# Reciprocal root mean squares by a full-precision matmul, a square root and a Newton step on every row

## Chip, cores and metric

The kernel runs on one core of a Trainium2 chip. The metric is the device time of one execution in microseconds. The time before is the median of three runs; one further execution was profiled, and all rows below come from it.

## What is computed

The reference is one inference step of a two-layer hybrid encoder for 1024 prompt tokens and 8 x 16 sample tokens, 1152 rows of width 1024. Layer 0 is attention, layer 1 a gated convolution; each is followed by a SwiGLU feed-forward block, and there is a final norm. The five norms are all of this form:

```
def rms_norm(x, g):
    xf = x.astype(jnp.float32)
    y = xf * lax.rsqrt(jnp.mean(xf * xf, axis=-1, keepdims=True) + EPS)
    return (y * g.astype(jnp.float32)).astype(x.dtype)
...
for i in range(DEPTH):
    hp = rms_norm(xp, norm_mix[i])
    ...  # attention (i = 0) or gated convolution (i = 1)
    xp = xp + mp
    xp = xp + swiglu(rms_norm(xp, norm_ffn[i]), w_ffn_gate[i], w_ffn_up[i], w_ffn_down[i])
y_prompt = rms_norm(xp, norm_final)
```

What matters here is the factor 1/sqrt(mean + EPS), one number per token. The kernel keeps activations transposed: features on the 128 partitions (eight tiles for 1024 features), tokens along the free dimension. So the mean of squares is a sum across partitions, and its root is needed on all 128 partitions, as a row of token factors that is the same on each.

## The kernel before, in words

All large products are done in three passes of a split format: `hi` and `lo` parts in fp32r, `hi*hi + hi*lo + lo*hi`. ScalarE makes `hi` (lines 187, 856), VectorE makes `lo` (lines 188, 857). A matmul group writes one PSUM bank; tags of banks are `g` (6) and `n` (2) after the attention, and `g` 2, `s` 3, `t` 2, `v` 1 in it (lines 714 and 1275).

**First norm** (lines 723 to 736): three blocks of 384 tokens. For each, eight tiles are loaded, split (`norm_tile`) and squared and added (`norm_sum`), and then `norm_end` makes the row of roots `rb`. The roots are applied after the projection (lines 328, 329, 348, 353), so products begin before the roots are there. The rotary tables are multiplied by them.

**Boundaries.** Between the attention output and the gates of layer 0, between the down projection and the convolution, and between the convolution's output and the gates of layer 1, `pairs` (line 1154) finishes x, makes the operands of the next products and squares x (`square`, line 929). Then `roots` (line 939) puts work into `self.late`, a list with a countdown in ticks; `tick` (line 163) is called once after each group of products. Sums come at tick 6, the spreading at tick 15.

The next products are in `unit` (line 995): two weight matrices at once by a seven-product scheme, for two halves s of the tokens, so 14 ticks per unit. The products are named by their right operand: `t2`, `b11`, `t1`, `b21`, `t3`, `b22`, `t4` (`ORDER`, line 969). In the first unit of a stage the root is not there yet, so the order is slightly different and the multiplication with the root (`rest`, line 1065) is put off until `spread` calls it, one tick into the second unit. Two wide tiles per half (`zg`, `zu`) hold a unit's result, with three buffers each. The copy of line 1037 writes into such a tile; the product `b21` writes to the same bank after that copy has read it.

**Last norm** (`down_last`, line 1224): blocks of 512, 384 and 256 tokens. After a block's eighth tile its root is made, with countdowns of 2 and 3 ticks for the first two blocks and at once for the last; `final` (line 1244) scales the eight tiles of the block and stores them.

How a root is made before: a matmul with a column of ones puts the sums with tokens on partitions (`sums`, line 233; one fp32 matmul per 128 tokens), VectorE makes the reciprocal root on a few columns by an integer guess and three Newton steps (`rstd`, line 240), the result is split and multiplied into identity matrices on ScalarE and GpSimd (`diagonals`, line 252; in `roots` lines 954 and 955), and two fp32r matmuls with ones spread the diagonals over all partitions (`spread`, line 271), from where ScalarE copies them (lines 227, 962). The per-head norm of the differential attention (`subln`, line 683) uses the same functions.

The order on each engine is not simply that of the source. The toolchain lays the instructions out ahead, by what it expects to be ready, and works in the order of the source where several are; on the chip each engine then keeps its order.

Of the kernel before, what the change touches and what calls it, by code (L numbers as in the profile page):

```python
# [11 lines left out]
F32 = mybir.dt.float32  # L12
F32R = mybir.dt.float32r
I32 = mybir.dt.int32
AF = mybir.ActivationFunctionType
ALU = mybir.AluOpType
# [3 lines left out]
P = 128  # L20
D = 1024
# [12 lines left out]
EPS = 1e-6  # L34
# [9 lines left out]
XW = SEQ + 2 + DB * (DS + 2)  # L44
PACE = 4.25
LAG = 8
SUMS = 6
SPREAD = 15
DLAG = 16
SLAG = 10  # L50
NLAG = 15
ETAG = {"sq": "ot", "ssq": "se", "diag": "pT", "rb": "rb"}
TURN = 6
RBUFS = {"st": 6, "k": 2, "q": 2, "v": 4, "pT": 2, "ot": 2, "kc": 1, "vc": 1, "se": 3, "os": 2, "ks": 1, "qbd": 2, "vn": 1,
         "smask": 1, "bmask": 1, "rb": 3}
# [44 lines left out]
class K:  # L100
# [24 lines left out]
    def early(self, name, dt=F32):  # L125

        return self.get(ETAG[name], name, (P, BLK), dt)

# [4 lines left out]
    def consts(self):  # L133
        nc, i, cp = self.nc, self.i, self.cp
        self.ident = cp.tile([P, P], F32, name="ident")
        make_identity(nc, self.ident)
        self.ones = cp.tile([P, 1], F32, name="ones")
        nc.vector.memset(self.ones, 1.0)
        self.onesr = cp.tile([P, P], F32R, name="onesr")
        nc.vector.tensor_scalar(self.onesr, self.ident, 0.0, 1.0, ALU.mult, ALU.add)  # L140
        self.g = cp.tile([P, 5, KT], F32, name="gains")
        nc.sync.dma_start(self.g, i["gains"])
        self.gn = cp.tile([P, 5, KT], F32, name="gainsn")
        nc.vector.tensor_scalar(self.gn, self.g, -1.0, None, ALU.mult)
# [47 lines left out]
    def norm_sum(self, st, m, b, xb):  # L192
        nc = self.nc
        tp = st["tmp"][b]
        sq = tp("sq")
        nc.scalar.activation(sq, xb, AF.Square)
        if st["new"] is None:
            nc.scalar.activation(xb, xb, AF.Copy, scale=self.g[:, st["gi"], m:m + 1])
        if st["acc"][b] is None:
            st["acc"][b] = sq  # L200
        else:
            acc = tp("ssq")
            nc.vector.tensor_tensor(acc, st["acc"][b], sq, ALU.add)
            st["acc"][b] = acc
        if m == KT - 1:
            if st["early"]:
                self.norm_end(st, b)()
            elif b < NB - 1:
                self.late.append([2, lambda: self.late.append([3, self.norm_end(st, b)])])
            else:  # L210
                rest = self.norm_end(st, b)
                while self.late:
                    self.late.pop(0)[1]()
                rest()

    def norm_end(self, st, b):

        tp = st["tmp"][b]
        n = st["acc"][b].shape[-1] // P
        ps = self.sums(st["pp"], st["tag"], st["acc"][b])  # L220
        r = self.rstd(ps[:, :n], D, *[self.tmp(t, (P, 4))[:, :n] for t in "vty"])
        dg = self.diagonals(r, tp)

        def rest():
            q = self.spread(st["pp"], st["tag"], dg)
            rb = st["rb"][b] = tp("rb")
            self.nc.scalar.copy(rb, q)
            if "then" in st:
                st["then"](b, q, rb)

        return rest

    def sums(self, pp, tag, sq):

# [595 lines left out]

    def small(self, name, n, dt=F32):

        bufs = {"sq": 4, "ssq": 4, "rb": 3, "diag": 2}[name]
        at = {"sq": 0, "ssq": 4, "rb": 8, "diag": 12}[name] + self.turn.get(name, 0) % bufs
        self.turn[name] = self.turn.get(name, 0) + 1
        t = self.bits[at // 2][:, at % 2 * HALF:at % 2 * HALF + n]
        return t if dt == F32R else t.bitcast(F32)
# [23 lines left out]

    def begin_sides(self, gi, pp, first, spill=False):

        return {"gi": gi, "pp": pp, "t": {}, "ssq": None, "first": first, "spill": spill, "split": None, "rest": None}

    def side(self, st, p, z, need=False):

# [70 lines left out]

    def roots(self, st):

        nc = self.nc

        def sums():
            ps = self.psum(st["pp"], "n")
            for j in range(9):
                nc.tensor.matmul(ps[:, j:j + 1], st["ssq"][:, j * P:(j + 1) * P], self.ones[:, 0:1], start=True, stop=True)
            r = self.rstd(ps[:, :9], D, *[self.tmp(t + "9", (P, 9)) for t in "vty"])
            parts = self.tmp("rp9", (P, 2, 9), F32R)
            nc.vector.tensor_copy(parts[:, 0], r)
            nc.vector.tensor_tensor(parts[:, 1], r, parts[:, 0].bitcast(F32), ALU.subtract)  # L950
            dg = [self.row("diag", F32R) for _ in range(2)]
            for j in range(9):
                c = slice(j * P, (j + 1) * P)
                nc.scalar.activation(dg[0][:, c], self.ident, AF.Copy, scale=parts[:, 0, j:j + 1].bitcast(F32))
                nc.gpsimd.tensor_scalar(dg[1][:, c], self.ident, parts[:, 1, j:j + 1].bitcast(F32), 1.0, ALU.mult, ALU.mult)
            self.late.append([SPREAD - SUMS, lambda: spread(dg)])

        def spread(dg):
            rb = st["rb"] = self.row("rb")
            for b in range(NB):  # L960
                c = slice(b * BLK, (b + 1) * BLK)
                nc.scalar.copy(rb[:, c], self.spread(st["pp"], "n", [t[:, c] for t in dg]))
            for do in st["rest"]:
                do(rb)

        self.late.append([SUMS, sums])


    ORDER = (("s2", "t2", "b"), ("a11", "b11", "a"), ("s1", "t1", "c"), ("a12", "b21", "a"), ("s3", "t3", "b"), ("s4", "b22", "c"), ("a22", "t4", "b"))
# [25 lines left out]
    def unit(self, pp, st, weights, by, end, last=False):  # L995

        nc = self.nc
        first = "rb" not in st
        if st["split"] is not None:
            split, raws = st["split"]  # L1000
            st["split"] = None
        else:
            split, raws = self.left_sides(*weights)
        order = self.ORDER
        zone, zg, zu = {}, [None, None], [None, None]
        tail = lambda s: slice(HALF + s * SUB, HALF + (s + 1) * SUB)
        vt = nc.vector
# [21 lines left out]
        for n in seq:  # L1029
            wn, p, zn = order[n]  # L1030
            for s in range(2):
                products(n, s, range(4) if not first or n > 2 else range(2 if n == 1 else 3, 4))
                ps = zone[zn, s]
# [30 lines left out]
        if first:  # L1064
            def rest(s, rb):
                nc.vector.tensor_tensor(zg[s], zg[s], self.cols(rb, s), ALU.mult)
                nc.gpsimd.tensor_tensor(zu[s], zu[s], self.cols(rb, s), ALU.mult)
                end(s, zg[s], zu[s])

            st["rest"] = [lambda rb, s=s: rest(s, rb) for s in range(2)]  # L1070
            st["rb"] = None

    def cols(self, t, s):

# [149 lines left out]
    def down_last(self, pp, x, wsrc, chunks):  # L1224

        nc, o = self.nc, self.o
# [7 lines left out]
        for j in range(KT // 2):  # L1234
            hi, lo = (self.take(n)[0][:, :2 * nk * P].rearrange("p (k c) -> p k c", c=P) for n in ("wh", "wl"))
            for z in range(2):
                w[j + 4 * z] = part = hi[:, z * nk:(z + 1) * nk, :], lo[:, z * nk:(z + 1) * nk, :]
                self.halve(*part, self.raw(wsrc[-1][j, z]))
        self.bits = [self.take("bits")[0] for _ in range(7)]
        cut = (0, 512, 896, T)  # L1240
        self.turn = {}
        st = self.begin_norm(4, None, pp, "n", {})
# [11 lines left out]
        for b in range(NB):  # L1254
            c = slice(cut[b], cut[b + 1])
            st["tmp"][b] = lambda name, dt=F32, n=cut[b + 1] - cut[b]: self.small(name, n, dt)
            for m in range(KT):
                ps = self.psum(pp, "g", (P, 512))[:, :cut[b + 1] - cut[b]]
# [147 lines left out]
```

## Time and profile before

| | us |
|---|---|
| median of 3 runs | 2657.38 |
| lowest, highest | 2656.47, 2662.86 |
| the profiled execution | 2656.52 |
| its span in the trace | 2654.7 |
| TensorE (PE) busy | 2590.6 |
| VectorE (DVE) busy | 1687.6 |
| ScalarE (ACT) busy | 944.9 |
| GpSimd (POOL) busy | 519.9 |
| mean granted TensorE clock | 0.992 of full speed |

Around the span lie 1.8 us. Busy times are of engines that run side by side; PE's matmuls overlap, so that the distance between the starts of two tells what one costs, and its duration tells less. The mean granted clock is an average over the span; a stretch at the lower level is seen only in a table by windows. In the order of time, the first norm lies in the first 56 us, the boundaries at about 713, 1488 and 1871 us, the last norm from 2610 us to the end.

### The profile page before, as it was taken

The page shows a single profiled execution, that of the slowest core. Times are in us where ns is not written, and L with a number is a line of the kernel's source. Part 1 is how long each engine was busy: PE and PEld are TensorE (multiplying, and loading weights), DVE is VectorE, ACT ScalarE, POOL GpSimd, SP SyncE. Part 2 cuts the span into 40 slices and gives each one's busy share as a digit, 9 for nine tenths or more (in the row PEclk, how much of TensorE's full clock was granted, in tenths as well). Part 3 has the DMA queues.
Part 4 walks back from the last instruction along what each step waited for, and adds up shares of the span by engine and source line. Part 5 has one row for each costly group of instructions (what it writes and reads, how often), then busy time and mean ns, then how long its engine had stood idle before and what let it go on. Part 6 is the DMA issues. An engine that isn't in the chain of part 4 may idle for free. (4 is left out here: it accounts for less than half of the span.)

```text
span 2654.7 us, 45342 instructions
## 1 busy us (share of the span) xinstructions
PE 2590.6 (98%) x17440; PEld 2548.5 (96%) x17440; DVE 1687.6 (64%) x3564; ACT 944.9 (36%) x1801; POOL 519.9 (20%) x621
## 2 busy tenths in 40 slices
PE   7999999999999999999999999999999999999997
PEld 6999999999899999999999999999999999999996
DVE  7667766677966666666326877777766666663325
ACT  6555445454532222233213422224422222222214
POOL 3434233321022222220000122210222222210002
PEclk9999999999999999999999999999999999999999
DMA  6655555662032222226212222262322222253211
GB/s 207 185 168 157 172 182 163 178 216 81 21 97 75 75 74 73 74 88 204 67 46 75 63 81 67 67 203 91 121 75 75 75 75 75 75 177 128 71 37 72
DMA packets 183577, 285.73 MB, mean 108 GB/s; under 512 B 38977, under 2 KB 107457, under 8 KB 183361
## 3 DMA queue, kind: packets, MB, share of 16 engines
q1 hardware_dynamic: 183360, 282.84, 33.6%
q8 instruction: 137, 2.24, 0.4%
q14 instruction: 80, 0.65, 0.1%
HBM read 206.67 MB, written 76.10 MB: 107 GB/s over the span
## 5 line engine op out<-in xcount | busy, mean ns | idle before, releaser
L856 ACT CAST h<-r 128x512 fp32r<-128x512 f32 x552 | 337.8, 618 | 1021.6 <-PE ps_g L1020 425.2
L857 DVE TENSOR_TENSOR l<-r,h 128x512 fp32r<-128x512 f32 x552 | 398.5, 725 | 137.2 <-ACT h L856 127.4
L1168 PE MATMUL ps_g<-yl,h 128*128 128x384 f32 x1152 | 387.7, 337 | 5.0 <-DVE yl L857 4.2
L1167 PE MATMUL ps_g<-yh,h 128*128 128x384 f32 x1152 | 387.2, 337 | 1.6 <-ACT yh L856 1.1
L1169 PE MATMUL ps_g<-yh,l 128*128 128x384 f32 x1152 | 386.9, 336 | 0.0
L1180 DVE TENSOR_TENSOR x<-ps_g,x 128x384 f32<-128x384 f32 x240 | 129.5, 553 | 211.5 <-PE ps_g L1169 211.1
L1052 POOL TENSOR_TENSOR g<-g,rb 128x288 f32<-128x288 f32 x98 | 82.1, 842 | 735.2 <-DVE g L1050 714.7
L1168 PEld LDWEIGHTS ps_g<-yl,h 128*128 128x128 f32 x1152 | 216.5, 188 | 6.9 <-DVE yl L857 6.8
L1167 PEld LDWEIGHTS ps_g<-yh,h 128*128 128x128 f32 x1152 | 216.6, 188 | 2.7 <-ACT yh L856 1.7
L1169 PEld LDWEIGHTS ps_g<-yh,l 128*128 128x128 f32 x1152 | 216.8, 188 | 0.0
L156 PE MATMUL ps_g<-hh,h 128*128 128x384 f32 x544 | 195.2, 359 | 12.7 <-ACT hh L187 6.9
L157 PE MATMUL ps_g<-hl,h 128*128 128x384 f32 x544 | 186.8, 343 | 0.6 <-DVE hl L188 0.6
L978 DVE TENSOR_TENSOR r<-r,r 128x512 f32<-128x512 f32 x224 | 153.3, 687 | 51.4 <-DMA r<-in_w_cin 22.5
L158 PE MATMUL ps_g<-hh,l 128*128 128x384 f32 x544 | 185.7, 341 | 0.0
L1056 POOL TENSOR_TENSOR u<-u,rb 128x576 f32<-128x576 f32 x98 | 156.0, 1592 | 111.5 <-DVE u L1008 107.4
L1086 DVE TENSOR_TENSOR g<-g,u 128x576 f32<-128x576 f32 x88 | 66.5, 758 | 120.1 <-POOL u L1056 120.1
L1008 DVE SCALAR_TENSOR_TENSOR u<-ps_g,u 128x288 f32<-128x288 f32 x224 | 100.2, 452 | 64.2 <-PE ps_g L1021 64.1
L1019 PE MATMUL ps_g<-tb21h,h 128*128 128x288 f32 x448 | 132.5, 296 | 5.4 <-ACT u L1037 5.4
L1019 PE MATMUL ps_g<-tt4h,h 128*128 128x288 f32 x448 | 132.2, 295 | 3.2 <-DVE u L1008 3.2
L1020 PE MATMUL ps_g<-tb11l,h 128*128 128x288 f32 x448 | 132.2, 295 | 1.6 <-DVE tb11l L886 1.6
L1019 PE MATMUL ps_g<-tt3h,h 128*128 128x288 f32 x448 | 133.6, 298 | 0.0
L1021 PE MATMUL ps_g<-tt3h,l 128*128 128x288 f32 x448 | 133.3, 298 | 0.0
(270 smaller groups left out, 7313.0 us busy)
## 6 DMA issues: line engine op xcount, KB each, us to landing
r<-in_w_gu SPq DMA_DIRECT2D x176, 256.0 KB, 2.7
y<-yd SPq DMA_DIRECT2D x52, 576.0 KB, 4.8
yd<-g SPq DMA_DIRECT2D x96, 288.0 KB, 2.6
r<-in_w_down SPq DMA_DIRECT2D x88, 256.0 KB, 2.6
r<-in_w_in SPq DMA_DIRECT2D x48, 256.0 KB, 3.4
r<-in_w_cin SPq DMA_DIRECT2D x48, 256.0 KB, 2.7
xd<-x SPq DMA_DIRECT2D x16, 576.0 KB, 3.0
x<-xd SPq DMA_DIRECT2D x16, 576.0 KB, 6.0
```

The costliest lines, as they stand in the source:

```text
L156: nc.tensor.matmul(ps, wh, xh, start=(j == 0), stop=False)
L157: nc.tensor.matmul(ps, wh, xl, start=False, stop=False)
L158: nc.tensor.matmul(ps, wl, xh, start=False, stop=(j == n - 1))
L856: self.nc.scalar.copy(hi, raw)
L857: self.nc.vector.tensor_tensor(lo, raw, hi.bitcast(F32), ALU.subtract)
L978: nc.vector.tensor_tensor(t, x_, y, ALU.add)
L1019: nc.tensor.matmul(ps, w[0][:, k, :], hi, start=(new and k == 0), stop=False, skip_group_check=True)
L1021: nc.tensor.matmul(ps, w[1][:, k, :], hi, start=False, stop=(k == 3), skip_group_check=True)
L1056: nc.gpsimd.tensor_tensor(zu[s], zu[s], self.cols(by()[1], s), ALU.mult)
L1167: nc.tensor.matmul(ps, w[q][0][:, e, :], ys[k][0][0][:, c], start=(k == 0), stop=False, skip_group_check=True)
L1168: nc.tensor.matmul(ps, w[q][0][:, e, :], ys[k][1][0][:, c], start=False, stop=False, skip_group_check=True)
L1169: nc.tensor.matmul(ps, w[q][1][:, e, :], ys[k][0][0][:, c], start=False, stop=(k == nk - 1), skip_group_check=True)
```

## The change

The sum of squares is multiplied by a 128x128 matrix of 1/1024 in a full-precision (fp32) matmul, which gives the mean on all partitions at once. ScalarE takes the square root of mean + EPS, VectorE its reciprocal r, and one Newton step follows: r * (1.5 - 0.5 * (mean + EPS) * r * r). All of it is done on whole rows of the block, 128 partitions by up to 512 tokens. `subln` keeps the old way. At a boundary the three blocks are done at tick 10, and `rest` is called at the end of the first unit. In the last norm, `final` is called by `norm_end` itself, the countdown of 3 is gone, and the last Newton operation of a block may write to PSUM, from where ScalarE copies it for GpSimd.

```
-SUMS = 6
-SPREAD = 15
+ROOTS = 10
...
+        self.over = cp.tile([P, P], F32, name="over")
+        nc.vector.memset(self.over, 1.0 / D)
+        self.eps = cp.tile([P, 1], F32, name="eps")
+        nc.vector.memset(self.eps, EPS)
...
             if st["early"]:
-                self.norm_end(st, b)()
+                self.norm_end(st, b)
             elif b < NB - 1:
-                self.late.append([2, lambda: self.late.append([3, self.norm_end(st, b)])])
+                self.late.append([2, lambda: self.norm_end(st, b)])
...
     def norm_end(self, st, b):
+        rb = st["rb"][b] = st["tmp"][b]("rb")
+        if "then" in st:
+            st["then"](b, self.root(st["pp"], st["tag"], st["acc"][b], rb, True), rb)
+        else:
+            self.root(st["pp"], st["tag"], st["acc"][b], rb)
+
+    def root(self, pp, tag, sq, r, spare=False):
+        nc = self.nc
+        ps, t = (self.psum(pp, tag, (P, 512))[:, :sq.shape[-1]] for _ in range(2))
+        nc.tensor.matmul(ps, self.over, sq, start=True, stop=True)
+        nc.scalar.activation(r, ps, AF.Sqrt, bias=self.eps[:, 0:1], scale=1.0)
+        nc.vector.reciprocal(r, r)
+        nc.vector.scalar_tensor_tensor(t, ps, EPS, r, ALU.add, ALU.mult)
+        nc.vector.scalar_tensor_tensor(t, t, -0.5, r, ALU.mult, ALU.mult)
+        q = ps if spare else r
+        nc.vector.scalar_tensor_tensor(q, t, 1.5, r, ALU.add, ALU.mult)
+        if spare:
+            nc.scalar.copy(r, q)
+        return q
...
     def roots(self, st):
         def sums():
-            ps = self.psum(st["pp"], "n")
-            for j in range(9):
-                nc.tensor.matmul(ps[:, j:j + 1], st["ssq"][:, j * P:(j + 1) * P], self.ones[:, 0:1], start=True, stop=True)
-            r = self.rstd(ps[:, :9], D, *[self.tmp(t + "9", (P, 9)) for t in "vty"])
...
             rb = st["rb"] = self.row("rb")
             for b in range(NB):
                 c = slice(b * BLK, (b + 1) * BLK)
-                nc.scalar.copy(rb[:, c], self.spread(st["pp"], "n", [t[:, c] for t in dg]))
-            for do in st["rest"]:
-                do(rb)
-        self.late.append([SUMS, sums])
+                self.root(st["pp"], "n", st["ssq"][:, c], rb[:, c])
+        self.late.append([ROOTS, sums])
...
-            st["rest"] = [lambda rb, s=s: rest(s, rb) for s in range(2)]
-            st["rb"] = None
+            for s in range(2):
+                rest(s, st["rb"])
```

## Rows read from the trace of the kernel before

**Rows 1.** The page's first part: busy time, share of the span, instructions.

```profile
PE 2590.6 (98%) x17440; PEld 2548.5 (96%) x17440; DVE 1687.6 (64%) x3564; ACT 944.9 (36%) x1801; POOL 519.9 (20%) x621
```

**Rows 2.** Waits of PE, 0 to 70 us: sum, times, longest.

```profile
PE ps_t L275 <- POOL diag L267: 3.4, 2, 2.2
PE ps_t L275 <- ACT diag L265: 2.1, 2, 1.6
```

**Rows 3.** Timeline of PE at B1: start, us, instruction, idle before and its releaser.

```profile
710.08 0.40 PE L1019 MATMUL ps_g<-tb21h,h 128*128 128x288 f32 x1 [2.34 <-ACT u L1037]
...
713.08 3.97 PE L946 MATMUL ps_n<-ones,ssq 128*128 128x1 f32 x18 [0.76 <-DVE ssq L937]
```

**Rows 4.** Table by windows at B1: busy time by engine, then the granted clock.

```profile
705.00:710.00 5.00, 2.45 (x17) 1.99 (x15) 5.00 (x7) 3.57 (x8) 0.00 (x0) 1.00 0.00 0
...
715.00:720.00 5.00, 5.00 (x23) 5.00 (x24) 1.72 (x7) 0.00 (x0) 0.00 (x0) 0.50 0.00 0
```

**Rows 5.** Timelines of PE and DVE in the tail, in order of time.

```profile
2634.16 0.89 PE L275 MATMUL ps_n<-bits,onesr 128*128 128x384 f32 x2 [1.35 <-ACT bits L265]
2635.60 3.80 DVE L1250 TENSOR_TENSOR x<-x,ps_n 128x384 f32<-128x384 f32 x8 [0.33 <-ACT bits L227]
2642.28 0.58 PE L237 MATMUL ps_n<-ones,bits 128*128 128x1 f32 x4 [3.58 <-DVE bits L203]
2647.66 1.74 DVE L1250 TENSOR_TENSOR x<-x,ps_n 128x256 f32<-128x256 f32 x5 [1.97 <-ACT bits L227]
```

**Rows 6.** Timeline of PE at B2.

```profile
1487.79 2.06 PE L946 MATMUL ps_n<-ones,ssq 128*128 128x1 f32 x18
1489.71 0.38 PE L1019 MATMUL ps_g<-tb21h,h 128*128 128x288 f32 x1
...
1496.17 0.29 PE L1019 MATMUL ps_g<-tb22h,h 128*128 128x288 f32 x1
...
1504.12 0.86 PE L275 MATMUL ps_n<-diag,onesr 128*128 128x384 f32 x4
...
1505.20 0.61 PE L275 MATMUL ps_n<-diag,onesr 128*128 128x384 f32 x2
1505.65 0.30 PE L1021 MATMUL ps_g<-tt2h,l 128*128 128x288 f32 x1
...
1514.96 0.29 PE L1019 MATMUL ps_g<-tb21h,h 128*128 128x288 f32 x1
```

**Rows 7.** Groups of instructions by line and shape: busy us, mean ns | idle before.

```profile
L638 PE MATMUL ps_s<-kc,qbd 128*32 128x256 f32 x128 | 10.8, 391 | 0.8 <-DMA kc<-in_ck 0.8
L156 PE MATMUL ps_g<-yh,wh 128*128 128x256 f32 x32 | 9.1, 283 | 0.0
L248 DVE TENSOR_TENSOR t<-t,v 128x9 f32<-128x9 f32 x9 | 1.4, 161 | 0.0
L353 DVE TENSOR_TENSOR z<-ps_g,rb 128x384 f32<-128x384 f32 x24 | 13.3, 553 | 3.2 <-PE ps_g L158 2.7
L1085 ACT ACT_TABLE_LOAD x1 | 1.3, 1283 | 0.0
```

**Rows 8.** Instructions of tile rc: duration ns min/median/max, first and last start.

```profile
L483 DVE RECIPROCAL rc<-sm x128: 144/162/167, 80.7 to 623.1; 128x1 f32<-128x1 f32 x128
...
L522 DVE TENSOR_TENSOR rc<-rc,lam x32: 140/159/915, 84.5 to 341.5; 128x1 f32<-128x1 f32 x32
```

**Rows 9.** B2: timelines of ACT and DVE, then busy time in one window.

```profile
1505.85 0.48 ACT L962 COPY rb<-ps_n 128x384 f32<-128x384 f32 x1 [0.32 <-PE ps_n L275]
1506.36 2.67 DVE L1066 TENSOR_TENSOR g<-g,rb 128x576 f32<-128x576 f32 x2 [2.36 <-ACT rb L962]
1511.11 0.40 ACT L1037 COPY u<-ps_g 128x288 f32<-128x288 f32 x1 [0.21 <-DVE xi L1112]
...
1494.25:1506.33 12.08, 12.08 (x90) 11.89 (x89) 7.70 (x22) 6.98 (x17) 4.02 (x9) 1.00 0.26 87
```

More of the change, by code (lines that the diff above doesn't have):

```diff
@@ L51 @@
 NLAG = 15
-ETAG = {"sq": "ot", "ssq": "se", "diag": "pT", "rb": "rb"}
+ETAG = {"sq": "ot", "ssq": "se", "rb": "rb"}
 TURN = 6
@@ L206, in norm_sum @@
             if st["early"]:
-                self.norm_end(st, b)()
+                self.norm_end(st, b)
             elif b < NB - 1:
-                self.late.append([2, lambda: self.late.append([3, self.norm_end(st, b)])])
+                self.late.append([2, lambda: self.norm_end(st, b)])
             else:
-                rest = self.norm_end(st, b)
                 while self.late:
                     self.late.pop(0)[1]()
-                rest()
+                self.norm_end(st, b)
     def norm_end(self, st, b):
[L218 to L231, printed above, removed]
+        rb = st["rb"][b] = st["tmp"][b]("rb")
[16 more added lines that the diff above has]
+        return q
     def sums(self, pp, tag, sq):
@@ L831, in small @@
     def small(self, name, n, dt=F32):
-        bufs = {"sq": 4, "ssq": 4, "rb": 3, "diag": 2}[name]
-        at = {"sq": 0, "ssq": 4, "rb": 8, "diag": 12}[name] + self.turn.get(name, 0) % bufs
+        bufs = {"sq": 4, "ssq": 4, "rb": 3}[name]
+        at = {"sq": 0, "ssq": 4, "rb": 8}[name] + self.turn.get(name, 0) % bufs
         self.turn[name] = self.turn.get(name, 0) + 1
@@ L862, in begin_sides @@
     def begin_sides(self, gi, pp, first, spill=False):
-        return {"gi": gi, "pp": pp, "t": {}, "ssq": None, "first": first, "spill": spill, "split": None, "rest": None}
+        return {"gi": gi, "pp": pp, "t": {}, "ssq": None, "first": first, "spill": spill, "split": None}
     def side(self, st, p, z, need=False):
@@ L939, in roots @@
     def roots(self, st):
-        nc = self.nc
         def sums():
-            ps = self.psum(st["pp"], "n")
-            for j in range(9):
-                nc.tensor.matmul(ps[:, j:j + 1], st["ssq"][:, j * P:(j + 1) * P], self.ones[:, 0:1], start=True, stop=True)
-            r = self.rstd(ps[:, :9], D, *[self.tmp(t + "9", (P, 9)) for t in "vty"])
[L948 to L958, printed above, removed]
             rb = st["rb"] = self.row("rb")
@@ L1004, in unit @@
         order = self.ORDER
+        if first:
+            st["rb"] = None
         zone, zg, zu = {}, [None, None], [None, None]
@@ L1238, in down_last @@
                 self.halve(*part, self.raw(wsrc[-1][j, z]))
-        self.bits = [self.take("bits")[0] for _ in range(7)]
+        self.bits = [self.take("bits")[0] for _ in range(6)]
         cut = (0, 512, 896, T)
```

## The prediction

> **What bounds the kernel now.** I read the page first: TensorE (PE) is busy 98% of the span, VectorE (DVE) 64% [rows 1]. So an engine matters only where it makes PE wait, or at the two ends, where PE has nothing to do. Four kinds of place are touched: the first norm, the three boundaries, the last norm, and the clock.
>
> The waits of PE in the first 70 us are the second view: the matmuls that spread the roots wait 3.4 us for GpSimd's half of the diagonals and 2.1 us for ScalarE's, 5.5 us in all [rows 2].
>
> Third, the boundaries. There are three: attention to gates (about 713 us, B1), down to conv (1488 us, B2), conv to gates (1871 us, B3). At B1 PE is already starved before the sums: 2.34 us of waiting in one place [rows 3], and 2.45 us of work in the five from 705 to 710 us, after which the granted clock is 0.50, the lower of the two levels, 1.2 instead of 2.4 GHz [rows 4]. At B2 and B3 PE has work throughout (a row for B2 comes below).
>
> Last, the tail: from the last sums (2642.28 us) to the last scaling (2647.66 us) runs a pure chain through DVE, ScalarE, GpSimd and PE [rows 5].
>
> **PE work at a boundary.** Removed at B2: the sums hold PE from 1487.79 us to the next product at 1489.71, 1.9 us; between 1504.12 and 1505.65 us the six spreading matmuls take 1.26 us beside two ordinary products [rows 6]. Together 3.1 us. Added: three fp32 matmuls of 384 columns. The trace has fp32 of 256 columns: two records each, 391 ns against 283 ns for an fp32r record of the same width [rows 7]. Two records at 0.117 + 0.108 us are 0.45 us, 0.67 us at 384 columns, so 2.0 us in all. Net -1.1 us at B2 and at B3. At B1 the sums took 3.97 us at the low clock, after a wait of 0.76 us [rows 3]. If other products now run at the low clock in their place, I gain 1.1 us; if not, 4.0 us. I take 2.0, nearer the first, since what starved PE before 711 us is untouched. Sum of this part: **-4.2 us**.
>
> **The path of the roots at a boundary.** Removed from DVE: 14 operations of 9 columns (0.16 us each [rows 7]), and nine diagonals each on ScalarE and GpSimd. Added to DVE, per block of 384: one reciprocal and three scalar-tensor-tensor operations. The latter are priced by the 128x384 operation from PSUM, 0.55 us each [rows 7]. The trace has reciprocals of one column only: median 162 ns, 159 ns for a product of one column, and minima of 144 and 140 ns [rows 8]. From below, a reciprocal is an ordinary operation, R = 0.55 us for 384 columns. From above: the slowest (167 ns) stands 8 ns over the median product, and were that all paid per column, 384 x 8 ns + 0.55 = 3.6 us. I take the 4 ns of the minima: R = 384 x 4 ns + 0.55 = **2.1 us**, for 256 columns about 1.45.
>
> When are the roots needed? Before the change, at B2, they are complete at 1505.85 + 0.48 = 1506.33 us; DVE waits 2.36 us for them. The rest of the first unit follows, frees its wide tiles, and the copy of the next unit's product ends at 1511.51 us; PE reads behind that copy at 1514.96 us, 3.45 us later [rows 6, 9]. With the change the tenth tick comes 1.9 us sooner than the trace has it (1496.17 us), at 1494.25, as the sums are gone, and PE is 1.1 us ahead. So the roots may come 12.1 + 3.45 - 1.1 = 14.4 us after the tick without PE waiting.
>
> How long will they take? First matmul, square root (priced as the 480 ns copy of the same shape [rows 9]) and handing over: 1.4 us. The tag has two banks, so a block's matmul must wait until the block before has read its sum: a period of R + 0.55 + 0.67 + 0.5 + 0.3 = R + 2.0 us, twice. Last block: R + 1.65 us. DVE's other work gets in between: it was busy 7.70 of the 12.08 us up to the roots, through which PE was busy without a gap [rows 9], about 6 us of it not the removed operations, and I charge half, 3.0 us. Sum: 3R + 10.0 = 16.4 us, 2.0 us too late. I use the same for B1 and B3: **+6.0 us** of PE waiting.
>
> The first unit's rest moves from the fifteenth tick to the end of that unit. It issues what it issued before: one DVE and one GpSimd product per half, Silu or the conv's products, and two stores on SP. In the program these now stand ahead of the second unit's weight loads, the place that every other unit's stores have, so I price it at nothing; the cover is the five raw buffers, and a late load would cost PE what the DMA takes.
>
> ScalarE gets a table load wherever Sqrt follows another table's function: about four in the first 80 us, one each at B1, B3 (for Silu) and the tail. The trace has two, 1.283 us each [rows 7]. ScalarE waits just ahead of most of these, so I count none. The Trainium skill ("ScalarE: Activation LUTs", What ACT_TABLE_LOAD costs) has 2.66 us with a drain, and advises batching by set; our row shows 1.283 and no drain. By the page one unhidden load per boundary would add 2.7 us each, by the row 1.3.
>
> **First norm.** The 5.5 us of waits end, and 1.0 us of spreading matmuls (six at 0.17 us start to start). What is late next: the last block's inputs and DVE, busy there and burdened by three times R + 1.65 us. I take **-4.0 us**, between 0 and -6.5.
>
> **Last norm.** PE's wait of 1.35 us for block 1's diagonals ends. Block 1's eight scalings on DVE (3.80 us, from 2635.60 us), which hold up the last additions, can start about two us sooner: matmul at 2627.3, +0.67 +0.5 +2.1, three operations with others between to 2633.3. The final chain was 5.4 us (2642.28 to 2647.66) [rows 5]; now fp32 matmul at the low clock 0.9, square root 0.5, R 1.45, three operations 1.4, the copy 0.4: 4.7 us. Block 0's longer DVE work and GpSimd's overlap may take some back: **-2.5 us**, between 0 and -4.
>
> **Sum.** -4.0 - 4.2 + 6.0 - 2.5 = -4.7 us on the profiled execution's 2656.5 us, so 2651.8. The median shown is 0.9 us higher, so I say **2652.5 us**. A measurement of this kernel can tell about 0.3%, 8 us, from no change; this is within it.
>
> **Rivals.**
>
> *Cheap reciprocals.* R = 0.55 us: the roots take 11.7 us, inside the 14.4, no waiting at the boundaries. Start -4.5, PE -4.2, tail -3.5: -12.2 us, **2645 us**. For it: the medians differ by 3 ns only. Against it: both minima and medians differ in the same direction.
>
> *Dear reciprocals, the slower end.* R = 3.6 us: the roots take 20.8 us after the tick, and PE waits 6.4 us at each boundary for the second unit's zones. It decides from R = 1.5 us, where 3R + 10.0 passes 14.4. Start -2.5, PE -4.2, waits +19.3, tail -1.5: +11.1 us, **2668 us**; a fall of the clock as at B1 would come on top. The Trainium skill ("VectorE: DVE Perf Modes", the walkthrough's section on the fixed hardware budget) says that Reciprocal runs an iterative divide with a repeat count of 8; no run here shows a wide one, and at eight cycles a column that is an estimate of 3.2 us, near this rival.
>
> *The banks stop PE.* PE works in order. If the second and third fp32 matmul stand right behind the first, each holds all products behind it until DVE has read the bank: 3.5 us and R + 2.0 - 0.67 = 3.4 us, 6.9 us per boundary in place of 2.0. Total about +10 us, **2668 us**, and up to 5 us more per boundary if the clock falls (ten us at half rate, as at B1). Against it: the third spreading pair at B2 was put behind two products [rows 6], so the order is laid out with the bank's release in view.
>
> **How the numbers follow.** Forecast 0.42, cheap 0.23, dear 0.20, banks 0.15. Faster than 2649.4 us: 0.30 of the forecast, 0.8 of cheap: 0.31. Slower than 2665.4 us: 0.07 of the forecast, 0.6 of dear, 0.65 of banks: 0.25. Same: the remaining 0.44. The range is 2641 to 2674 us: it leaves out the best of cheap reciprocals with a full gain at the start, and the falls of the clock at all boundaries.
>
> **What would show it.** A 128x384 reciprocal of 2.1 us and one of 1.45 us at 256; rb complete about 16 us after tt3's last product at B2 and B3; PE waiting some 2 us for the copy at the second unit's tb21 or for a bank; no wait at the matmuls of the first norm; last scaling some 2.5 us sooner, against the end of the products. I am wrong if the reciprocal is beyond 3 us, if PE stops at the fp32 matmuls themselves, or if a low clock follows a boundary other than B1.

## The result, and the profile after

The changed kernel takes **2686.91 us** (median of 6 runs, 2685.06 to 2691.07) where the kernel before, on the same chip, takes 2656.93 us (2651.16 to 2662.86): a ratio of 1.0119, 95% interval 1.0106 to 1.0131, or 30 us more. The prediction was 2652.5 us, within 2641 to 2674. The profiled execution took 2685.66 us (span 2683.9 us) against 2656.52 us (span 2654.7 us) before.

The page's first part says almost nothing of it. To be read against [rows 1]:

```profile
PE 2591.2 (97%) x17350; PEld 2539.8 (95%) x17350; DVE 1727.5 (64%) x3500; ACT 943.0 (35%) x1767; POOL 497.0 (19%) x576
```

TensorE's work is the same within 0.6 us; DVE has 40 us more and still reads 64%. The new operation itself, by its line (columns: count, duration in ns as minimum, median and maximum, first and last start, shapes):

```profile
L233 DVE RECIPROCAL rb<-rb x12: 2537/2552/2555, 17.8 to 1905.1; 128x384 f32<-128x384 f32 x12
L233 DVE RECIPROCAL bits<-bits x3: 1754/2540/3343, 2642.8 to 2673.2; 128x512 f32<-128x512 f32 x1, 128x384 f32<-128x384 f32 x1, 128x256 f32<-128x256 f32 x1
```

A 128x384 reciprocal takes 2.55 us, where I had taken 2.1. Now who waits. TensorE's waits over the whole span (sum, times, longest):

```profile
PE ps_g L1012 <- ACT h L865: 17.3, 5, 6.2
...
PE ps_g L1014 <- DVE l L866: 7.2, 3, 2.6
...
PE ps_n L231 <- DVE bits L206: 6.4, 2, 5.3
```

The first two are new, one long and one shorter wait at each boundary: 24 us. L865 and L866 are the two halves of a split weight, `h` and `l`. So TensorE doesn't wait for roots, or for anything that a root holds up. It waits for *weights*. The timeline of PE at B2 says which (start, us, instruction, and the idle time before it with its releaser):

```profile
1497.54 0.81 PE L231 MATMUL ps_n<-ssq,over 128*128 128x384 f32 x2
...
1505.67 0.81 PE L231 MATMUL ps_n<-ssq,over 128*128 128x384 f32 x2
...
1511.23 0.81 PE L231 MATMUL ps_n<-ssq,over 128*128 128x384 f32 x2
...
1518.38 0.61 PE L1012 MATMUL ps_g<-tt2h,h 128*128 128x288 f32 x1 [4.88 <-ACT h L865]
...
1524.25 0.61 PE L1014 MATMUL ps_g<-tt2h,l 128*128 128x288 f32 x1 [2.62 <-DVE l L866]
```

TensorE goes through the three fp32 matmuls without a wait. It stops at the products with `tt2`: the first of the second unit, whose weight `s2` is a sum of three blocks that DVE must add (L969) before ScalarE can cast it (L865) and DVE can split off the rest (L866). DVE's timeline in the same stretch shows what these adds stand behind:

```profile
1501.79 2.54 DVE L233 RECIPROCAL rb<-rb 128x384 f32<-128x384 f32 x1
...
1505.11 0.68 DVE L969 TENSOR_TENSOR r<-r,r 128x512 f32<-128x512 f32 x1
...
1507.13 2.55 DVE L233 RECIPROCAL rb<-rb 128x384 f32<-128x384 f32 x1
...
1512.69 2.55 DVE L233 RECIPROCAL rb<-rb 128x384 f32<-128x384 f32 x1 [0.47 <-ACT rb L232]
...
1515.93 0.68 DVE L969 TENSOR_TENSOR r<-r,r 128x512 f32<-128x512 f32 x1
...
1517.00 0.68 DVE L969 TENSOR_TENSOR r<-r,r 128x512 f32<-128x512 f32 x1
...
1518.18 2.65 DVE L1059 TENSOR_TENSOR g<-g,rb 128x576 f32<-128x576 f32 x2
...
1523.51 2.72 DVE L866 TENSOR_TENSOR l<-r,h 128x512 fp32r<-128x512 f32 x3
```

The first add runs between the first two reciprocals, the other two only behind the third. The splits `l` come after the first unit's rest and its products. ScalarE's casts follow at once on the last add, and it had stood idle for it:

```profile
1517.71 1.66 ACT L865 CAST h<-r 128x512 fp32r<-128x512 f32 x3 [5.05 <-DVE r L969]
```

Last, the table by windows of the same stretch (busy time of PE, PEld, DVE, ACT and POOL, granted clock, DMA share, GB/s), beside that of the kernel before in the stretch that answers to it:

```profile
1500.00:1505.00 5.00, 5.00 (x39) 5.00 (x39) 5.00 (x8) 2.00 (x4) 0.00 (x0) 1.00 0.01 3
...
1510.00:1515.00 5.00, 3.50 (x24) 3.00 (x22) 4.52 (x6) 0.58 (x1) 0.00 (x0) 1.00 0.00 0
1515.00:1520.00 5.00, 1.62 (x7) 1.62 (x8) 4.97 (x9) 1.66 (x3) 1.68 (x1) 0.59 0.00 0
1520.00:1525.00 5.00, 2.38 (x10) 2.04 (x10) 5.00 (x9) 0.00 (x0) 3.55 (x3) 0.50 0.02 0
1525.00:1530.00 5.00, 5.00 (x24) 5.00 (x23) 4.00 (x4) 0.00 (x0) 1.47 (x2) 0.55 0.18 12
```

```profile
1485.00:1490.00 5.00, 5.00 (x43) 5.00 (x42) 5.00 (x9) 4.21 (x8) 0.00 (x0) 1.00 0.02 3
1490.00:1495.00 5.00, 5.00 (x40) 5.00 (x39) 4.66 (x16) 1.42 (x4) 0.00 (x0) 1.00 0.00 0
1495.00:1500.00 5.00, 5.00 (x39) 5.00 (x39) 4.07 (x16) 2.62 (x9) 1.15 (x4) 1.00 0.16 52
1500.00:1505.00 5.00, 5.00 (x39) 5.00 (x37) 3.23 (x6) 2.73 (x8) 2.87 (x6) 1.00 0.30 107
```

After, DVE is busy nearly throughout while PE starves, and behind PE's waits the granted clock goes to the lower level, as it did only at B1 before [rows 4]. In the fifteen us from 1515 to 1530 the clock was at the lower level for some nine tenths of the time (mean 0.55), and PE was busy for 9.0 us (1.62 + 2.38 + 5.00); at the upper level that work would have taken about 4 us less. This is an estimate from the table; with the 7.5 us of the two waits it about makes up what B2 loses. Before, DVE was full up to 1490 us and had 3.0 us idle in the fifteen after (0.34 + 0.93 + 1.77). An engine that is busy for 64% of the span has almost no room in the very stretch into which the change puts its work.

Where the 29.2 us of the span come from can be read from ScalarE's copy of `u`, the first in a stage's first unit and the first in its third, in both timelines. For B2, before and after (start, us, instruction):

```profile
1489.01 0.67 ACT L1037 COPY u<-ps_g 128x288 f32<-128x288 f32 x2
...
1531.15 0.40 ACT L1037 COPY u<-ps_g 128x288 f32<-128x288 f32 x1 [1.11 <-PE ps_g L1021]
```

```profile
1498.76 0.67 ACT L1030 COPY u<-ps_g 128x288 f32<-128x288 f32 x2
...
1552.43 0.40 ACT L1030 COPY u<-ps_g 128x288 f32<-128x288 f32 x1 [1.12 <-PE ps_g L1014]
```

The stage behind B1 starts 5.0 us late; its first two units take 51.9 us before and 58.6 after (+6.7). At B2 it is 42.1 and 53.7 (+11.5), at B3 43.4 and 52.9 (+9.5); between the boundaries 3.7 us come back, and the rest of the span adds 0.2. The boundaries make 27.7 us; the start makes 5.0, or less than that in the median, as the experiments show.

### The profile page after: what moved, and what is told of

Its sections match the earlier page's. It is cut to its first block, busy times and chain, and to the rows that moved or that the text cites. A ratio compares the mean times of both kernels' runs of the same rounds, so it can differ in the third digit from the quotient of the medians.

```text
span 2683.9 us, 45002 instructions
## 1 busy us (share of the span) xinstructions
PE 2591.2 (97%) x17350; PEld 2539.8 (95%) x17350; DVE 1727.5 (64%) x3500; ACT 943.0 (35%) x1767; POOL 497.0 (19%) x576
## 5 line engine op out<-in xcount | busy, mean ns | idle before, releaser
L865 ACT CAST h<-r 128x512 fp32r<-128x512 f32 x552 | 337.3, 618 | 1035.1 <-PE ps_g L1013 429.5
L866 DVE TENSOR_TENSOR l<-r,h 128x512 fp32r<-128x512 f32 x552 | 398.0, 726 | 142.4 <-ACT h L865 132.1
L969 DVE TENSOR_TENSOR r<-r,r 128x512 f32<-128x512 f32 x224 | 153.0, 687 | 59.2 <-DMA r<-in_w_gu 27.7
L1012 PE MATMUL ps_g<-tt2h,h 128*128 128x288 f32 x448 | 135.4, 303 | 17.1 <-ACT h L865 17.1
L1014 PE MATMUL ps_g<-tt2h,l 128*128 128x288 f32 x448 | 134.4, 302 | 7.2 <-DVE l L866 7.2
L1013 PE MATMUL ps_g<-tt2l,h 128*128 128x288 f32 x448 | 135.1, 302 | 0.0
```

Source lines behind the costliest of these rows:

```text
L865: self.nc.scalar.copy(hi, raw)
L866: self.nc.vector.tensor_tensor(lo, raw, hi.bitcast(F32), ALU.subtract)
L1012: nc.tensor.matmul(ps, w[0][:, k, :], hi, start=(new and k == 0), stop=False, skip_group_check=True)
L1013: nc.tensor.matmul(ps, w[0][:, k, :], lo, start=False, stop=False, skip_group_check=True)
L1014: nc.tensor.matmul(ps, w[1][:, k, :], hi, start=False, stop=(k == 3), skip_group_check=True)
```

## Experiments

The theory is that the reciprocals' time on DVE, put ahead of the second unit's weights, starves TensorE at the boundaries (**theory 1**). Against it stood: ScalarE's queue, with square roots that wait for banks (**theory 2**); the prediction's own path, late roots (**theory 3**); and the place of the first unit's rest. All ratios are to the kernel before, on the same chip. Its medians there were 2656.0 to 2658.9 us, so medians of kernels measured on different chips compare only to about 3 us, and the ratios are the better guide. The column "boundaries" is the time of the first two units of each stage, measured as above, less that of the kernel before (51.9, 42.1, 43.4 us).

| kernel | median us | ratio (95%) | boundaries B1, B2, B3, us |
|---|---|---|---|
| changed kernel | 2686.91 | 1.0119 (1.0106–1.0131) | +6.7, +11.5, +9.5 |
| ends_new | 2657.41 | 1.0001 (0.9991–1.0010) | -0.2, -0.1, -0.1 |
| mid_new | 2680.66 | 1.0096 (1.0077–1.0115) | +8.6, +10.7, +9.4 |
| rest_back | 2684.94 | 1.0104 (1.0087–1.0120) | +7.9, +8.7, +8.3 |
| mid_norecip | 2657.83 | 1.0004 (0.9995–1.0013) | -4.7, +0.9, -1.4 |
| recips_1of3 | 2665.05 | 1.0022 (1.0012–1.0031) | -2.1, +6.5, +0.6 |
| recips_2of3 | 2683.03 | 1.0095 (1.0079–1.0112) | +4.6, +8.7, +8.3 |
| recip_beside | 2695.62 | 1.0155 (1.0141–1.0169) | +9.8, +13.9, +10.9 |
| chain_pool | 2661.04 | 1.0025 (1.0013–1.0036) | -2.7, +3.6, 0.0 |
| roots_apart | 2693.55 | 1.0145 (1.0131–1.0159) | +7.5, +13.9, +10.2 |
| sums_first | 2673.60 | 1.0059 (1.0045–1.0073) | -0.9, +14.4, +1.1 |
| rsqrt | 2640.17 | 0.9940 (0.9928–0.9953) | -3.1, +0.8, -1.4 |
| rsqrt_plain | 2639.44 | 0.9927 (0.9913–0.9941) | -5.0, -0.9, -1.4 |

**The parts alone.** `ends_new` is the changed kernel with the boundaries' old code; to make room, its sums are taken with ones and the 1/1024 is put into the square root and the Newton step. `mid_new` is the kernel before with the changed boundaries.

```diff
 # ends_new, against the changed kernel
-ROOTS = 10
+SUMS = 6
+SPREAD = 15
-        nc.tensor.matmul(ps, self.over, sq, start=True, stop=True)
-        nc.scalar.activation(r, ps, AF.Sqrt, bias=self.eps[:, 0:1], scale=1.0)
+        nc.tensor.matmul(ps, self.onesr.bitcast(F32), sq, start=True, stop=True)
+        nc.scalar.activation(r, ps, AF.Sqrt, bias=self.eps[:, 0:1], scale=1.0 / D)
...
 # mid_new, against the kernel before
+                self.root(st["pp"], "n", st["ssq"][:, c], rb[:, c])
+        self.late.append([ROOTS, sums])
...
+            for s in range(2):
+                rest(s, st["rb"])
```

> The new roots at the first and the last norm only; the three boundaries as before. Set against each other, the two traces put about +5 us of the change before the first boundary (2.6 us in the first 80 us, 2.4 us behind a fall of the clock at 565 us), +23.6 us at the three boundaries and +0.6 us in the tail. If the parts add up, this kernel takes about 5.6 us more than the kernel before (2662 us, ratio 1.002). If the prediction's prices for the two ends were right (-4.0 and -2.5 us), it takes 2650 us.

> The new roots and the moved rest at the three boundaries only; first and last norm as before. If the parts add up as the traces read: +23.6 us, 2680 us, ratio 1.009, with TensorE waiting 5 to 6 us for the second unit's first product at each boundary, and the clock at 0.50 behind it. If the loss was the whole change's new order, laid out anew by the toolchain, and not the boundaries' own work, it takes less than 2668 us.

Measured: 2657.41 and 2680.66 us, +0.7 and +24.0 us. The two ends together are nothing; neither the 5.6 us read from one execution nor the 6.5 us gain forecast. The boundaries make 24 of 30 us; the parts add up to 24.7, with an interval for the boundaries of 1.0077 to 1.0115 (20 to 31 us).

**Without the boundary reciprocals.**

```diff
-    def root(self, pp, tag, sq, r, spare=False):
+    def root(self, pp, tag, sq, r, spare=False, inv=True):
-        nc.scalar.activation(r, ps, AF.Sqrt, bias=self.eps[:, 0:1], scale=1.0)
-        nc.vector.reciprocal(r, r)
+        nc.scalar.activation(r, ps, AF.Sqrt, bias=self.eps[:, 0:1], scale=1.0 if inv else 1e-9)
+        if inv:
+            nc.vector.reciprocal(r, r)
...
+                self.root(st["pp"], "n", st["ssq"][:, c], rb[:, c], inv=False)
```

> The changed kernel with the reciprocals at the three boundaries left out (nine instructions; the square root is scaled so that the values stay small). Theory 1: the wide reciprocals take VectorE's time from the second unit's sums and splits, so without them (3 x 2.55 us less at each boundary) TensorE's wait for the first of those products falls from 5 to 6 us to under 1.5 us, the clock stays up at the second and third boundary, and the time falls by 15 us or more, to 2672 us or less. Theory 2: it is ScalarE, whose casts stand behind square roots and table loads that wait for banks: these waits stay, and the time falls by 5 us or less. Theory 3, my prediction's path (late roots hold the first unit's tiles): the roots come 7.6 us sooner, TensorE's wait for the roots goes, but the wait at the second unit's first product stays.

Measured: 2657.83 us. Without nine instructions of 2.55 us, 23 us of 1727 on DVE, the 29 us are gone. Square roots, table loads, fp32 matmuls and Newton steps stand as they did. The waits on split weights fall from 24.5 us to 0.5 us in the whole span:

```profile
PE ps_g L1013 <- ACT h L866: 0.5, 2, 0.3
```

But the nine are also in the roots' chain, so theory 3 isn't out yet.

**The reciprocals on other data, and the delay without the reciprocals.** The first puts the reciprocals back on DVE but on other data, the second puts a delay of the same length back into the roots' chain but on GpSimd.

```diff
 # recip_beside, against mid_norecip
+        else:
+            nc.vector.reciprocal(sq, sq)
 # chain_pool, against mid_norecip
+        else:
+            for _ in range(4):
+                nc.gpsimd.tensor_scalar(r, r, 1.0, 1.0, ALU.mult, ALU.mult)
```

> As the kernel without the boundary reciprocals (2657.8 us), but VectorE runs a reciprocal of the same 128x384 shape for each block all the same, on the squares, which nobody reads afterwards: VectorE's load is that of the changed kernel, while no root waits for it through its own data. If it is VectorE's time and order that is lost (the second unit's sums and splits stand behind reciprocals), the loss comes back: 2678 us or more, with TensorE waiting 4 us or more for the second unit's first product. If it is the length of the roots' own chain, the time stays at 2658 us, within 5.

> As the kernel without the boundary reciprocals, but in place of each reciprocal four plain 128x384 operations on GpSimd, about 0.6 us each, so that each block's root takes as long as with its reciprocal (some 2.6 us and the handing over) while VectorE is free. If VectorE's time is what is lost, the time stays at 2658 us, within 5. If it is the length of the roots' chain (late roots, a bank held longer, ScalarE's square roots waiting for it), it comes to 2675 us or more.

Measured: 2695.62 and 2661.04 us. With the reciprocals on data that nobody reads, the loss is back, and 9 us more than in the changed kernel. So nobody has to need their result for it. The roots are late all the same, as they stand behind these reciprocals on DVE (19.6 us at B2 from the first matmul, at 1506.93, to the last operation); it is the second kernel that parts delay from load. TensorE's wait at B2 for the second unit's first product is now 10.81 us:

```profile
1533.69 0.61 PE L1015 MATMUL ps_g<-tt2h,h 128*128 128x288 f32 x1 [10.81 <-ACT h L868]
```

With the delay on GpSimd, the roots come as late as in the changed kernel. At B2, matmul of the first block, the last block's stay on GpSimd, and the last operation of the roots:

```profile
1487.79 0.81 PE L231 MATMUL ps_n<-ssq,over 128*128 128x384 f32 x2
```

```profile
1503.71 3.10 POOL L237 TENSOR_SCALAR rb<-rb 128x384 f32<-128x384 f32 x4 [2.59 <-ACT rb L232]
```

```profile
1508.28 0.55 DVE L241 SCALAR_TENSOR_TENSOR rb<-ps_n,rb 128x384 f32<-128x384 f32 x1
```

That is 21.0 us from the matmul to the end (1508.83), against 20.6 in the changed kernel (1497.54 to 1518.15) and 15.3 in `mid_norecip`. It costs 4 to 6 us over `mid_norecip` (4 by the medians against the kernel before, 6 by the ratios and by the boundaries), not 29. So theory 3 falls as the cause of the loss. What it does cost shows at a later fp32 matmul of each boundary, which waits for the bank until DVE has read an earlier sum: 2.00 us at B2, at the third one, and 4.5 us in the whole span.

```profile
1501.77 1.23 PE L231 MATMUL ps_n<-ssq,over 128*128 128x384 f32 x2 [2.00 <-DVE ps_n L238]
```

Theory 2's waits are there too: ScalarE's square roots wait 21.0 us for their sums in the whole span, 30.1 in the changed kernel, 10.2 in `mid_norecip`. Half of the rise from 10.2 to 30.1 is in this kernel, and with it the whole cost is no more than those 4 to 6 us. What counts is DVE's time.

**How many of them.** The reciprocals of the first one and the first two blocks of three are kept.

```diff
-                self.root(st["pp"], "n", st["ssq"][:, c], rb[:, c], inv=False)
+                self.root(st["pp"], "n", st["ssq"][:, c], rb[:, c], inv=b < 1)
```

(`b < 2` in the second kernel.)

> The changed kernel with the reciprocal kept in the first block of 384 columns at each boundary and left out in the other two (their square root scaled to stay small). None of three costs 2657.8 us, all three 2687 us. If VectorE is full at the boundary, each microsecond given to a reciprocal comes out as a microsecond or more of TensorE's waiting from the first one on: a straight line, 2667 us. If VectorE has idle time there that takes the first reciprocals up, it stays below 2661 us.

> As above with the reciprocals of two blocks of three kept. On a straight line 2677 us; if idle time takes up the first two and only the third is paid for, below 2668 us.

Measured: 2657.8, 2665.1, 2683.0, 2686.9 us for none to three, not all on the same chip; by the ratios the steps are about 5, 19 and 6 us. Neither the straight line nor a free first one. By boundary it reads better: at B3 the first reciprocal costs 2.0 us and the second 7.7; at B2 the first costs 5.6, and TensorE's waits there are again for split weights of the second unit (1.76 and 2.80 us). In the steps that are well above 2.55 us the granted clock falls as well (at B3, from 1895 to 1915 us with one reciprocal, the mean is 1.00, from 1900 to 1920 us with two 0.74); how much of a step is the clock was not measured.

**Place in the program.** First the rest, then the roots spread over the unit.

```diff
 # rest_back
-            for s in range(2):
-                rest(s, st["rb"])
+            self.late.append([1, lambda: [rest(s, st["rb"]) for s in range(2)]])
 # roots_apart
-ROOTS = 10
+ROOTS = (3, 7, 11)
...
+        for b in range(NB):
+            self.late.append([ROOTS[b], lambda b=b: block(b)])
```

> The changed kernel with the first unit's rest put back to one tick into the second unit, behind that unit's loads and sums in the program, as it was before; the new roots stay at tick 10. If the rest's place makes the loss (its products stand ahead of the second unit's sums and wait for the roots), the time falls by 8 us or more, below 2679 us. If the root operations themselves take the time, it stays within 4 us of the changed kernel's 2687 us.

> The changed kernel with the same operations, but the roots of the three blocks set at ticks 3, 7 and 11 of the first unit instead of all three at tick 10. If the loss is VectorE's queue in the stretch around the unit change, where three reciprocals stand within 11 us ahead of the second unit's sums, spreading them over the unit gives most of it back: 2670 us or less. If any 7.6 us more of VectorE's work at a boundary costs what it does, wherever it stands, the time stays within 5 us of 2687.

Measured: 2684.94 us, 2 us less, which the intervals don't tell from nothing. In the trace the second of the two waits at each boundary shrinks, from 2.3 to 2.6 us to 0.9 to 1.1 us, as the splits `l` no longer stand behind the rest: the move of the rest, which I had priced at nothing, is at most a small part. And 2693.55 us: spreading the roots makes it worse by 7 us, against what I expected. At B2 the windows show PE starved twice. First it waits at the first unit's `tb21` for ScalarE's copy of `u`, 2.86 us where it waited 0.84 us in the changed kernel; the copy now stands behind the table load and the square root (1.28 and 0.58 us, from 1504.23 us).

```profile
1506.96 0.40 PE L1012 MATMUL ps_g<-tb21h,h 128*128 128x288 f32 x1 [2.86 <-ACT u L1030]
```

Then it waits at the second unit, as in the changed kernel and for longer:

```profile
1505.00:1510.00 5.00, 3.04 (x15) 3.04 (x16) 5.00 (x7) 2.54 (x6) 0.00 (x0) 0.77 0.00 0
...
1520.00:1525.00 5.00, 2.76 (x21) 2.52 (x20) 5.00 (x9) 0.00 (x0) 0.68 (x1) 0.98 0.00 0
1525.00:1530.00 5.00, 0.00 (x0) 0.00 (x0) 5.00 (x8) 0.00 (x0) 2.88 (x3) 0.50 0.00 0
```

An earlier place is no emptier on DVE: it is where that engine had no idle time before the change either (1485 to 1490 us above).

**The second unit's sums ahead of the roots.**

```diff
+        self.late.append([ROOTS, lambda: st.update(split=self.left_sides(*st["next"]))])
         self.late.append([ROOTS, sums])
...
 # in gates(), and in conv() with its own two weights
+        st["next"] = weights(1)
```

> The changed kernel, all its operations kept, with the second unit's weight loads, sums and first splits put ahead of the roots in the program (at the same tick 10), where they stood behind them. If what is lost is the order (sums queued behind reciprocals although VectorE had room for both), the wait for the second unit's first product goes and the time falls to 2672 us or less. If it is the amount of VectorE's work in a stretch where it has no idle time left, TensorE waits elsewhere (for the rest, for the roots, at the next unit) and the time stays within 6 us of 2687.

Measured: 2673.60 us, between the two cases, and the boundaries say why: at B1 and B3 the loss is nearly gone (-0.9 and +1.1 us in place of +6.7 and +9.5; -4.7 and -1.4 without reciprocals). So at two boundaries it was mostly the order: DVE's work fits if the sums go first. At B2 nothing is won. The +14.4 us overstate it, as the copy that ends the measure comes late there; over the whole stage, from the first copy at B2 to the first at B3, this kernel takes 390.9 us, the changed one 391.5 and the kernel before 381.7. TensorE no longer waits for the second unit's first product, but 2.15 us at its `tb21` and 3.38 us at the third unit's first product:

```profile
1526.75 0.40 PE L1013 MATMUL ps_g<-tb21h,h 128*128 128x288 f32 x1 [2.15 <-ACT u L1031]
...
1541.46 0.61 PE L1013 MATMUL ps_g<-tt2h,h 128*128 128x288 f32 x1 [3.38 <-ACT h L865]
```

The first of these is the prediction's own path: the copy waits until the first unit's rest has gone through DVE's `xi`.

```profile
1526.30 0.40 ACT L1031 COPY u<-ps_g 128x288 f32<-128x288 f32 x1 [7.50 <-DVE xi L1108]
```

From 1500 to 1530 us DVE is busy for 29.4 of the thirty. Ahead of the second wait the third unit's sums come behind the taps of the convolution, which DVE has at B2 alone (L1125, 1.27 to 1.39 us each), and the last of them also behind an `xi` that waits 1.30 us for GpSimd. So the amount of DVE's work counts at B2, but no run parts it from the order there.

**The root without a reciprocal.** ScalarE has a function that gives the reciprocal square root at once; the Newton step refines it. The second kernel leaves the Newton step out.

```diff
 # rsqrt
-        nc.scalar.activation(r, ps, AF.Sqrt, bias=self.eps[:, 0:1], scale=1.0)
-        nc.vector.reciprocal(r, r)
+        nc.scalar.activation(r, ps, AF.Abs_reciprocal_sqrt, bias=self.eps[:, 0:1], scale=1.0)
 # rsqrt_plain, besides
-        nc.vector.scalar_tensor_tensor(t, ps, EPS, r, ALU.add, ALU.mult)
-        nc.vector.scalar_tensor_tensor(t, t, -0.5, r, ALU.mult, ALU.mult)
...
-        nc.vector.scalar_tensor_tensor(q, t, 1.5, r, ALU.add, ALU.mult)
```

> The changed kernel with ScalarE's reciprocal square root in place of square root and reciprocal, at all five norms; the Newton step stays. VectorE has twelve reciprocals less (30.6 us, 15 of them in boundaries and tail's stretches that count). If the reciprocals are the whole loss at the boundaries, these cost nothing or a little less than before (-4.2 us of TensorE's work by my sum), and at the ends up to 2.5 us each is gained: 2645 to 2657 us. If ScalarE's part (table loads, banks) has a price of its own, it stays above 2660 us.

> The kernel with ScalarE's reciprocal square root (2640.2 us) without its Newton step: three operations of 0.55 us less on VectorE per block at all five norms, and one copy less on ScalarE in the last. If VectorE still sets the boundaries, each gives up to 5 us: 2625 to 2630 us. If without the reciprocals TensorE is the bound there again, only the two ends gain, 1 to 2 us each at most: 2636 to 2640 us.

Measured: **2640.17 us**, ratio 0.9940 (0.9928 to 0.9953), which beats both kernels, by 16 and 47 us; and 2639.44 us without the Newton step, no gain that can be told. The function takes what the square root took (582 ns):

```profile
L232 ACT ACTIVATE rb<-ps_n,eps x9: 580/582/583, 707.6 to 1871.7; 128x384 f32<-128x384 f32 x9
```

In the profiled execution the 15.5 us of its span come from the start (the stage behind B1 begins 6.3 us sooner), the boundaries (-3.7) and the tail (-5.8); what lies between gives back 0.3. Without the Newton step the profile shows another 3.6 us less at the boundaries and 2.9 us less in the tail, and a start that is 8.0 us later (below); the medians are equal. So the 15 us that three boundaries still bound by VectorE would have given aren't there.

## Why the prediction was wrong

**The step that failed is "The path of the roots at a boundary".** It took DVE's new operations as a delay of the roots and asked who waits for roots. From that came its +6.0 us of waiting at three boundaries; measured are +27.7 us, with TensorE's own savings already taken off. It charged "DVE's other work" half of 6 us, 3.0 us, as something that makes the roots late. It never asked the other way round: what the reciprocals make late. In the program that is the second unit's sums; and they have a consumer with no slack. `chain_pool` shows how wrong the question was: roots as late as those of the changed kernel, 21 us behind the first matmul where I had allowed 14.4 us, cost 4 to 6 us in all in place of 30. `recip_beside` shows the other half: reciprocals whose result nobody needs, and a loss of 40 us. The path itself is real: with the sums out of the way, in `sums_first`, TensorE waits 2.15 us at the second unit's `tb21` at B2, about the 2.0 us forecast there. It is a small cost that a larger one hid.

The sum was there to be made from the trace of before. Added per boundary: 3 x (2.55 + 3 x 0.55) = 12.6 us on DVE; removed: 14 x 0.16 = 2.2 us; net +10.4 us. Idle on DVE from 1475 to 1515 us: 6 us, by the table of windows before (busy 34.0 of 40), and not all in the right place. With my own R of 2.1 us it would have been +9.0 us: too much as well. Without reciprocals it is +2.7 us, which fits, as `mid_norecip` shows. The sum is a warning and no price: at B1 and B3 the same work nearly fits once the sums stand first.

Point by point:

- *R = 2.1 us*: 2.55 us measured, 1.75 for 256 columns where I had 1.45. Between my forecast and the "dear" rival, and no large part of the error: put into my own 3R + 10.0 it gives 17.7 us, a wait of 3.3 us per boundary, and 2656 us in all.
- *PE work, -4.2 us*: about right. Without the reciprocals the boundaries give -5.2 us together (-4.7, +0.9, -1.4). It came mostly at B1, where I had said 1.1 to 4.0; fp32 of 384 columns takes 0.81 us for its two records.
- *PE waits for late roots, +6.0 us*: with PE's own work the boundaries make +27.7 us where I had +1.8, by another mechanism, and at another product than the `tb21` that I named.
- *The low clock at B1 only*: it follows B2 and B3 as well (0.50 in the window above; at B3 a mean of 0.66 from 1905 to 1920 us). That was one of the things I said would prove me wrong.
- *The banks stop PE*: not in the changed kernel; no wait at the second and third fp32 matmul at B2. With the roots delayed on GpSimd they do, by 4.5 us in all.
- *The rest's move and ScalarE's table loads at nothing*: about right for this kernel, by `rest_back` and `mid_norecip`. Five loads at 1.283 us stay in `rsqrt` too, and cost nothing that shows; in `roots_apart` one of them holds up a copy that TensorE waits for.
- *First norm, -4.0 us*: the waits for diagonals are gone, but DVE, 16.12 us busy of the twenty from 20 to 40 us before, is then full, and PE waits for its next inputs (L370, L357) instead. The same window before and after, then two waits of the kernel after:

```profile
20.00:40.00 20.00, 17.84 (x95) 17.31 (x94) 16.12 (x49) 15.20 (x33) 6.28 (x6) 0.91 0.65 217
```

```profile
20.00:40.00 20.00, 17.77 (x94) 15.58 (x93) 19.48 (x36) 14.71 (x31) 2.41 (x2) 1.00 0.65 208
```

```profile
PE ps_g L159 <- DVE z L370: 6.0, 2, 3.5
PE ps_t L400 <- DVE z L357: 2.3, 1, 2.3
```

  The same error in small. How much of the 5.0 us at B1's start is the first norm's is open: profiled executions with wide reciprocals there begin that stage 4.6 to 10.9 us late, those with the reciprocal square root at -6.3 and +1.7, `mid_new` with the old first norm at +0.1, but the medians of `ends_new` and before are equal.
- *Last norm, -2.5 us*: +0.4 us. Block 1's reciprocal and its eight scalings (2.54 and 3.80 us) stand ahead of the last additions on DVE, and the last matmul waits for these:

```profile
2671.47 1.22 PE L231 MATMUL ps_n<-bits,over 128*128 128x256 f32 x2 [5.34 <-DVE bits L206]
```

```profile
2659.18 2.54 DVE L233 RECIPROCAL bits<-bits 128x384 f32<-128x384 f32 x1
...
2665.19 3.80 DVE L1243 TENSOR_TENSOR x<-x,ps_n 128x384 f32<-128x384 f32 x8
...
2673.24 1.75 DVE L233 RECIPROCAL bits<-bits 128x256 f32<-128x256 f32 x1 [1.82 <-ACT bits L232]
...
2676.83 1.75 DVE L1243 TENSOR_TENSOR x<-x,ps_n 128x256 f32<-128x256 f32 x5 [0.44 <-ACT bits L239]
```

  From that matmul to the last scaling it is 5.36 us, as before [rows 5]; I had 4.7. With `rsqrt` it is 3.10 us, and the wait 2.75 instead of 5.34:

```profile
2629.03 0.70 PE L231 MATMUL ps_n<-bits,over 128*128 128x256 f32 x2 [2.75 <-DVE bits L206]
```

- *The rivals*: "dear reciprocals" had the right sign and the right instruction, with a price of 11 us, since it too counted only the delay of the roots.

What stays open: why B2 pays for the very first reciprocal and the steps from none to three are so uneven, and where up to 4 us come back between the boundaries. A version with the sums first at B1 and B3 and the wide reciprocals kept was not tried beyond `sums_first`.

## What to carry to other kernels

An operation added to an engine can cost twice: as a delay to whoever waits for its result, and as a delay to all that stands behind it on that engine. Read the engine's idle time in the very stretch, not its share of the span, and add up the new work against it before asking about latency. The sum warns, but the order decides as well: here two boundaries of three lost mostly by it. When the work doesn't fit, first put what the bounding engine needs ahead of it, and better still find a form of it on an engine that is idle there.

## What the runs showed of the hardware

- A reciprocal on DVE costs by the column: 1754 ns for 256 columns, 2552 for 384, 3343 for 512, so 6.2 ns per column and some 160 ns besides. By that, one of a single column takes about what an ordinary operation takes, as seen in [rows 8]. A scalar-tensor-tensor operation of 384 columns takes 0.55 us, so the reciprocal is nearly five of them. The Trainium skill ("VectorE: DVE Perf Modes", the walkthrough's section on the fixed hardware budget) calls it an iterative divide with a repeat count of 8. The trace agrees that a wide one costs several ordinary operations; the estimate of 3.2 us that I drew from the page is a quarter above the 2.55 us measured.
- ScalarE's reciprocal square root takes 582 ns for 128x384, as long as its square root.
- Four GpSimd operations of 128x384 with two constants take 2.94 to 3.10 us, longer than one reciprocal of that shape on DVE (2.55 us); at the boundaries nine sets of four cost 4 to 6 us where nine reciprocals cost 29.
